# Mixer weights in sections of 512 columns through all ring tiles, parameters earlier on SyncE's queue, narrow products in one run

## The chip, the cores and the metric

The kernel runs on one core of a Trainium2 chip. The metric is device time in microseconds. The runs of the kernel before took 1303.86, 1306.07 and 1306.61 us; the median is 1306.07.

## The reference, cut to what matters

One sequence of 256 tokens, width 1024, with 16 meta tokens in front, goes through a first block (a mixer and a mixture of experts) and then a second block of two layers. The change touches the first block's mixer alone:

```python
a = rmsnorm(h, g_mix)
proj = a @ w_in                       # 1024 x 3584: seven sections of 512 columns
sb_q, sb_k, sb_v, hg_q, hg_f, hg_i, hg_g = split(proj)
o_sb = merge_heads_norm(stick_breaking_attention(sb_q, sb_k, sb_v), sb_gain)
log_f = log(lb + (1 - lb) * sigmoid(hg_f)); k_in = (1 - lb) * sigmoid(-hg_f)
o_hg = merge_heads_norm(hgrn2(silu(hg_q), k_in, hg_i, log_f), hg_gain) * silu(hg_g)
h = h + concat(o_sb, o_hg) @ w_out    # 1024 x 1024
m = rmsnorm(h, g_ffn)
h = h + moe(m)                        # 32 experts: gate, up 1024 x 512; down 512 x 1024
```

Everything is float32. The weights of the 32 experts are 201 MB and all are read.

## The kernel before, in words

**Engines and order.** The program is written in Python on a layer that puts in the semaphores and orders the instructions of each engine by priority and readiness; `tc.issue_after(i)` adds an order behind an instruction. A DMA waits on the queue of the engine that issues it (SyncE, `nc.sync`, for nearly all) until the place of its destination is free, and what is behind it on that queue waits too.

**Places for weights.** `K.ring` is a pool of four tiles of 128 x 4096 floats (2 MB); `wtile()` (L53) takes the next. Five further "boost" tiles (`boost`, L249) are opened one after the other as the mixer's memory comes free: the first at once, the second when `p3` closes (`hg_done`, L570), the third when `p4` closes (L593), two more when `p2` has closed and the `w_out` loop is at n = 3.

**Expert stream.** `expert_stream` (L663) lists all expert loads of 2 MB in the order of use; `fetch(n)` (L685) issues those up to number n, `take()` issues one more and hands out the next. Loads 3 to 7 go to boost tiles, load 9 (RING + BOOST) to a spare tile, load 13 (`mem`) to a pool of its own, all others to the ring.

**Mixer weights.** One ring tile, `qtile`, holds four quarters of 512 KB. A quarter is 128 columns of a `w_in` section (rows of 512 bytes), for sections 2 and 5 two blocks of 128 rows with 512 columns (2 KB), for `w_out` one block of 128 rows (4 KB). `refill` (L125) issues the next quarter. `weights()` (L158) splits quarter after quarter into a high part (a ScalarE cast, L74) and the rest (VectorE or, for `POOLED`, GpSimd, L75), then refills; at the quarters of `AHEAD` it also fetches expert loads 1 to 4. `parts()` hands out one split and has the next one made. Sections come in the order 4, 3, 6, 0, 1, 2, 5.

**Products.** `proj_T` (L281) handles five sections: per 128 columns 24 products of the split weights with the split activations `ah`, `al`. `proj_N` (L296) handles sections 2 and 5: in each of four turns and for each of two blocks kk, 12 wide products (512 columns) and then four narrow ones of the meta tokens (`am`, 32 columns of weights, each with two records in the trace) with the unsplit weights `wt`, added over eight blocks into four regions of the bank `pm`. After each piece `fill()` runs the next bit of `work`: the bias table (`biases`, L1216, which ends in a store of 2.3 MB, `skew`, on ScalarE's queue), the levels of hgrn2 (`lev_prep`, `lev_mm`) and the stick-breaking attention (`sb_z`, `sb_corr`, `sb_exp`, `sb_pv`).

**Small parameters.** `prm` (four small vectors), `rb` and `oh` are loaded on SyncE's queue into tiles of pool `a2`, which opens after the norm (L238 to 246); `parameters()` (L262) transposes `prm` on TensorE after the first piece's products. `cmk` (the level masks) is also loaded on SyncE's queue (L349).

## Time and profile before

| | |
|---|---|
| median of 3 runs | 1306.07 us |
| profiled execution | 1305.46 us |
| its span, first to last instruction | 1303.8 us |
| TensorE (matmul) busy | 1097.9 us, 84% |
| VectorE / ScalarE / GpSimd busy | 641.0 / 454.1 / 65.2 us |
| moved by DMA | 336.54 MB, mean 258 GB/s |
| mean granted TensorE clock | 0.941 |

The profile of one execution has a page of totals, views that group instructions or waits, and timelines. In a timeline a row is one instruction or several alike in a row: start in us from the span's start, length, engine (PE is TensorE, PEld its weight loads, DVE VectorE, ACT ScalarE, POOL GpSimd, SP SyncE; a q behind it means its queue, where DMAs are issued), line, operation, out<-in tiles, shape, count, and in brackets the idle time before it and what ended that. In the view of stretches each engine's busy time stands with the number of its instructions, then the granted clock as a share of full speed, the mean busy share of 16 DMA engines, and GB/s.

### The profile page before, as it was taken

The numbers are of one execution on the slowest core, as the hardware profiler recorded it, in microseconds if no ns is written. First come the engines' busy times: TensorE is split into PE (matmuls) and PEld (weight loads), VectorE is DVE, ScalarE is ACT, GpSimd is POOL, SyncE is SP. The second block draws the span as 40 slices with busy tenths as digits, with TensorE's granted clock in tenths as the row PEclk, the third lists the DMA queues.
The fourth block names the chain that finished last, engine by engine and source line by source line (L and its number), as shares of the span: only waits on it lengthen the run. The fifth ranks groups of instructions, "written<-read, shape, count | busy, mean of one in ns | idle before, by whom it ended". The sixth has DMA issues, their size and how long they took to land. (4 is left out here: it accounts for less than half of the span.)

```text
span 1303.8 us, 18742 instructions
## 1 busy us (share of the span) xinstructions
PE 1097.9 (84%) x7773; PEld 798.5 (61%) x7773; DVE 641.0 (49%) x1225; ACT 454.1 (35%) x808; POOL 65.2 (5%) x109
## 2 busy tenths in 40 slices
PE   8859998767565756646589899999999999999997
PEld 7856674314121412101058668999998887999996
DVE  6646355311021101101037876877677766886676
ACT  5526542101001000000035564444453654544442
POOL 7201000000000000000000001000001000000001
PEclk9979999988888888888799999999998999999999
DMA  8676677999999999999999105555446334365430
GB/s 219 148 173 234 226 292 288 403 406 408 409 409 405 409 409 409 409 409 409 409 370 351 66 4 191 201 219 195 162 151 210 121 133 175 124 243 192 184 118 33
DMA packets 132593, 336.54 MB, mean 258 GB/s; under 512 B 4837, under 2 KB 41294, under 8 KB 132504
## 3 DMA queue, kind: packets, MB, share of 16 engines
q1 hardware_dynamic: 128796, 327.32, 66.4%
q10 hardware_dynamic: 1724, 2.95, 1.8%
q0 software_dynamic: 1984, 5.04, 1.3%
q8 instruction: 62, 1.02, 0.3%
q14 instruction: 27, 0.22, 0.0%
HBM read 331.88 MB, written 3.41 MB: 257 GB/s over the span
## 5 line engine op out<-in xcount | busy, mean ns | idle before, releaser
L75 DVE TENSOR_TENSOR wl<-wt,wh 128x1024 fp32r<-128x1024 f32 x212 | 258.0, 1219 | 111.1 <-ACT wh L74 106.1
L74 ACT CAST wh<-wt 128x1024 fp32r<-128x1024 f32 x216 | 223.9, 1042 | 179.4 <-PE ps L48 134.4
L48 PE MATMUL ps<-xl,wh 128*128 128x256 f32 (+1 forms) x912 | 255.7, 280 | 2.2 <-DVE xl L1434 1.8
L48 PE MATMUL ps<-xh,wh 128*128 128x256 f32 (+1 forms) x912 | 257.0, 282 | 0.4 <-ACT xh L1097 0.3
L48 PE MATMUL ps<-xh,wl 128*128 128x256 f32 (+1 forms) x912 | 255.3, 280 | 0.0
L48 PE MATMUL ps<-wt,xe 128*32 128x512 f32 x944 | 138.9, 720 | 94.9 <-DMA wt<-in_w_expert_up_dram 57.4
L48 PEld LDWEIGHTS ps<-xl,wh 128*128 128x128 f32 (+1 forms) x912 | 171.2, 188 | 4.4 <-POOL xl L1434 2.2
L48 PEld LDWEIGHTS ps<-xh,wh 128*128 128x128 f32 (+1 forms) x912 | 171.2, 188 | 3.4 <-issue 0.8
L48 PEld LDWEIGHTS ps<-xh,wl 128*128 128x128 f32 (+1 forms) x912 | 171.0, 188 | 0.1
L48 PEld LDWEIGHTS ps<-wt,xe 128*32 128x32 f32 x944 | 28.3, 122 | 194.7 <-DMA wt<-in_w_expert_up_dram 73.8
L48 PE MATMUL ps<-wt,hT 128*32 128x512 f32 x496 | 78.6, 766 | 54.0 <-DMA wt<-in_w_expert_down_dram 48.4
L1006 DVE TENSOR_TENSOR hs<-hs,ps 128x512 f32<-128x512 f32 x8 | 5.5, 688 | 224.4 <-PE ps L48 216.0
L1028 DVE TENSOR_TENSOR h<-h,ps 128x512 f32<-128x512 f32 x32 | 22.0, 687 | 145.2 <-PE ps L48 145.2
L48 PEld LDWEIGHTS ps<-wt,hT 128*32 128x32 f32 x496 | 15.6, 129 | 106.5 <-DMA wt<-in_w_expert_down_dram 68.1
L1005 ACT ACTIVATE hs<-ps 128x512 f32<-128x512 f32 x8 | 4.8, 597 | 184.4 <-PE ps L48 184.4
L48 PE MATMUL ps<-wh,gh 128*128 128x512 f32 x176 | 68.6, 390 | 0.0
L48 PE MATMUL ps<-wh,gl 128*128 128x512 f32 x176 | 68.5, 389 | 0.0
L48 PE MATMUL ps<-wl,gh 128*128 128x512 f32 x176 | 68.4, 389 | 0.0
L1040 ACT COPY ye<-ps 128x512 f32<-128x512 f32 x14 | 8.2, 586 | 161.9 <-PE ps L48 161.9
L48 PE MATMUL ps<-ah,wh 128*128 128x256 f32 (+1 forms) x160 | 43.2, 302 | 14.4 <-ACT wh L74 13.9
L2006 ACT CAST gh<-cv 128x256 fp32r<-128x256 f32 x44 | 17.9, 407 | 74.7 <-DVE cv L2003 74.7
L48 PE MATMUL ps<-al,wh 128*128 128x256 f32 (+1 forms) x160 | 42.6, 298 | 0.0
(478 smaller groups left out, 1688.1 us busy)
## 6 DMA issues: line engine op xcount, KB each, us to landing
wt<-in_w_expert_gate_dram SPq DMA_DIRECT2D x30, 2048.0 KB, 17.4
wt<-in_w_expert_down_dram SPq DMA_DIRECT2D x30, 2048.0 KB, 17.9
wt<-in_w_expert_up_dram SPq DMA_DIRECT2D x29, 2048.0 KB, 17.0
wt<-in_ffn_w_in_dram SPq DMA_DIRECT2D x20, 2048.0 KB, 7.8
wt<-in_ffn_w_out_dram SPq DMA_DIRECT2D x10, 2048.0 KB, 10.3
wt<-in_w_in_dram SPq DMA_DIRECT2D x28, 512.0 KB, 3.8
bt<-in_w_expert_up_dram SPq DMA_DIRECT2D x3, 2048.0 KB
wt<-in_shared_w_kv_dram SPq DMA_DIRECT2D x3, 2048.0 KB, 13.5
```

Source lines behind the costliest of these rows:

```text
L48: return nc.tensor.matmul(o, a, b, start=start, stop=stop, skip_group_check=True)
L74: nc.scalar.copy(wh, src)
L75: on.tensor_tensor(out=wl, in0=src, in1=wh.bitcast(F32), op=ALU.subtract)
L1005: nc.scalar.activation(hs, pgu[0], AF.Silu)
L1006: V.tensor_tensor(out=hs, in0=hs, in1=pgu[1], op=ALU.mult)
L1028: V.tensor_tensor(out=hs_, in0=hs_, in1=py, op=ALU.add)
L1040: nc.scalar.copy(ye[:, hf], pd[hf])
L2006: nc.scalar.copy(gh, c)
```

## The change

The mixer's weights come in whole sections of 512 columns (one ring tile each, 2 MB; the first in two halves, `w_out` in two tiles of two loads each) and pass through all four ring tiles; `section()` issues one, four at the start and one more whenever the four pieces of a section have been split. A helper `chain` issues these, `gm`, the small parameters and the first ten expert loads on SyncE's queue in the order written. The small parameters are asked for behind the first half section, into a tile that shares the place of `qT`. Expert load 0 goes to the first boost tile behind the fourth section; 2, 4, 5, 6 go to the other boost tiles (`BOOSTED`) and 1, 3, 7, 8 to the ring. `cmk` is loaded from ScalarE's queue. In `proj_N` the narrow products of all eight blocks stand in one run behind all wide ones; in `sb_corr` and `sb_pv` the narrow products of both halves likewise.

```diff
--- before.py
+++ after.py
@@ -17,7 +17,6 @@
 DRAM = bass.MemoryType.DRAM
 D = 1024
-AHEAD = (18, 21, 23, 25)
 POOLED = (0, 12, 14, 16)
 EPS = 1e-6
 LEVELS = (64, 32, 16, 8, 4, 2, 1)
@@ -81,6 +80,16 @@
         for _ in range(n):
             mm(ps[:, 384:512], K.ident, K.ident, True, True)
+    loads = []
+
+    def chain(dst, src):
+
+        with ExitStack() as es:
+            if loads:
+                es.enter_context(tc.issue_after(loads[-1]))
+            loads.append(nc.sync.dma_start(dst, src).ins)
+
+    K.chain = chain
     K.nbehind = 0
     K.pulse = pulse
     K.mm, K.bank, K.wtile, K.rpow, K.split = mm, bank, wtile, rpow, split
@@ -108,7 +117,7 @@
     nc.scalar.preload_act_table_set("sigmoid_and_others")
     expert_stream(K)
     gm = e1.tile([8, 128], F32, name="gm")
-    nc.sync.dma_start(gm, I["g_mix"].rearrange("o (c p) -> (o c) p", p=128))
+    K.chain(gm, I["g_mix"].rearrange("o (c p) -> (o c) p", p=128))
     rb = a1.tile([33, NH], F32, name="rb")
     V.memset(rb, 1e30)
@@ -116,22 +125,39 @@
     w_out = I["w_out"][0].rearrange("(k p) f -> p k f", p=128)
-    quarters = [w_in[:, :, 512 * s + 128 * c:512 * s + 128 * c + 128] if s not in (2, 5) else
-                w_in[:, 2 * c:2 * c + 2, 512 * s:512 * s + 512] for s in (4, 3, 6, 0, 1, 2, 5) for c in range(4)]
-    quarters += [w_out[:, k:k + 1] for k in W_OUT]
-    qtile = K.wtile()
-    views, loads = [], []
-
-    def refill():
-        n = len(views)
-        if n < len(quarters):
-            q = quarters[n]
-            v = qtile[:, 1024 * (n % 4):1024 * (n % 4) + 1024].rearrange("p (a b) -> p a b", a=q.shape[1])
-            loads.append(nc.sync.dma_start(v, q))
-            views.append(v)
-
-    for _ in range(4):
-        refill()
+
+    views = []
+    chain = K.chain
+    small = a1.tile([128, 4, 256], F32, name="small", tag="qT").rearrange("p a b -> p (a b)")
+    prm, oh = small[0:24, 0:128], small[0:33, 256:640]
+
+    def parameters_in():
+        for o, n, src in ((0, 8, "lb_logits"), (8, 4, "sb_gain"), (12, 4, "hg_gain"), (16, 8, "g_ffn")):
+            chain(prm[o:o + n], I[src].rearrange("o (c p) -> (o c) p", p=128))
+        chain(rb[0:32], I["rel_bias_2"])
+        chain(oh, I["c_rel"])
+
+    def section():
+        n = len(views) // 4
+        t = K.wtile()
+        if n < 7:
+            s = (4, 3, 6, 0, 1, 2, 5)[n]
+            v = t.rearrange("p (k f) -> p k f", k=8)
+            src = w_in[:, :, 512 * s:512 * s + 512]
+            for cs in ((slice(0, 256), slice(256, 512)) if n == 0 else (slice(0, 512),)):
+                chain(v[:, :, cs], src[:, :, cs])
+                if cs.start == n == 0:
+                    parameters_in()
+            views.extend(v[:, 2 * c:2 * c + 2] if s in (2, 5) else v[:, :, 128 * c:128 * c + 128] for c in range(4))
+        else:
+            v = t.rearrange("p (k f) -> p k f", k=4)
+            for j in range(2):
+                k = W_OUT[4 * (n - 7) + 2 * j]
+                chain(v[:, 2 * j:2 * j + 2], w_out[:, k:k + 2])
+            views.extend(v[:, k] for k in range(4))
+
+    for _ in range(2):
+        section()
     negtri = a1.tile([128, 128], F32, name="negtri")
@@ -159,11 +185,11 @@
         for n in range(28):
             v = views[n]
             yield split(v, v.shape[1:], on=nc.gpsimd if n in POOLED else V), v
-            if n < 20:
-                refill()
-            if n in AHEAD:
-                with tc.issue_after(loads[-1].ins):
-                    K.fetch(AHEAD.index(n) + 1)
+            if n % 4 == 3:
+                if n < 23:
+                    section()
+                else:
+                    K.fetch(2 if n == 23 else 4)
         yield None
     stream = weights()
@@ -236,20 +262,17 @@
     mixh, mixl = ah[:, :, 16:272], al[:, :, 16:272]
     a2 = p2.enter_context(tc.tile_pool(name="a2", bufs=2))
-    prm = a2.tile([24, 128], F32, name="prm", tag="wA")
-    oh = a2.tile([33, 384], F32, name="oh", tag="wB")
     ohr = a2.tile([33, 384], F32R, name="ohr", tag="wA")
     tb = a2.tile([NH, 384], F32, name="tb", tag="wB")
-    for o, n, src in ((0, 8, "lb_logits"), (8, 4, "sb_gain"), (12, 4, "hg_gain"), (16, 8, "g_ffn")):
-        nc.sync.dma_start(prm[o:o + n], I[src].rearrange("o (c p) -> (o c) p", p=128))
-    nc.sync.dma_start(rb[0:32], I["rel_bias_2"])
-    nc.sync.dma_start(oh, I["c_rel"])
+    for _ in range(2):
+        section()
     K.boost, K.boostp = ExitStack(), []
     def boost(n):
         K.boostp += n * [K.boost.enter_context(tc.tile_pool(name=f"boost{len(K.boostp)}", bufs=n, side="right"))]
     boost(1)
+    K.fetch(1)
     p3, p4 = ExitStack(), ExitStack()
     a3 = p3.enter_context(tc.tile_pool(name="a3", bufs=1, side="right"))
@@ -298,8 +321,10 @@
         V.memset(dstm, 0.0)
         po = [bank() for _ in range(2)]
         pm = bank()
+        wts = []
         for kp in range(4):
             (wh, wl), wt = parts()
+            wts.append(wt)
             for kk in range(2):
                 k = 2 * kp + kk
                 for t in range(2):
@@ -307,13 +332,13 @@
                     mm(po[t], ah[:, k, ts], wh[:, kk], k == 0, False)
                     mm(po[t], al[:, k, ts], wh[:, kk], False, False)
                     mm(po[t], ah[:, k, ts], wl[:, kk], False, k == 7)
-                for j in range(4):
-                    mm(pm[32 * j:32 * j + 32, 0:128], am[:, k], wt[:, kk, 128 * j:128 * j + 128], k == 0, k == 7)
-            refill()
             if kp < 3:
                 fill()
         for t in range(2):
             nc.scalar.copy(dst[:, t], po[t])
+        for k in range(8):
+            for j in range(4):
+                mm(pm[32 * j:32 * j + 32, 0:128], am[:, k], wts[k // 2][:, k % 2, 128 * j:128 * j + 128], k == 0, k == 7)
         for j in range(4):
             V.tensor_copy(dstm[32 * j:32 * j + 32, j], pm[32 * j:32 * j + 32, 0:128])
         fill()
@@ -346,7 +371,7 @@
     proj_T(16, evac_silu(hq))
     proj_T(16, evac_silu(sg))
     cmk = a3.tile([128, 7, 64], F32, name="cmk")
-    nc.sync.dma_start(cmk, I["c_lev"].rearrange("p (l j) -> p l j", l=7))
+    nc.scalar.dma_start(cmk, I["c_lev"].rearrange("p (l j) -> p l j", l=7))
     with tc.issue_after(getattr(last[-1], "ins", last[-1])):
         tab = nc.scalar.preload_act_table_set("natural_log_exp_and_others")
@@ -523,6 +548,7 @@
                 mm(zA[u].rearrange("p (i t) -> p i t", i=2)[:, :, 128:256], negone,
                    spB[u][:, 0:256].rearrange("p (i t) -> p i t", i=2), False, True)
                 mm(zB[u][:, 0:256], negtri, spB[u][:, 0:256], False, True)
+            for u in range(2):
                 for i in range(2):
                     cs = slice(32 * (2 * qd + i), 32 * (2 * qd + i) + 32)
                     mm(zB[u][cs, ci], negone[:, 0:32], spA[u][:, 256 * i:256 * i + 256], False, False)
@@ -561,8 +587,10 @@
                 for u in range(2):
                     hd = 2 * c + u
                     mm(o_[u][:, 128:256], sv[:, 1, 64 * hd:64 * hd + 64], wB[u][:, 128 * i:128 * i + 128], False, False)
+            for i in range(2):
                 for u in range(2):
-                    mm(o_[u], svm[qs, c, 64 * u:64 * u + 64], wB[u][qs, ci], False, True)
+                    mm(ob[64 * u:64 * u + 64, 256 * i:256 * i + 256], svm[qs, 2 * qd + i, 64 * u:64 * u + 64],
+                       wB[u][qs, ci], False, True)
             return norm_mix(nc, bank, mm, a2, ob, bd64, epsr, [sbg[:, 2 * qd + i:2 * qd + i + 1] for i in range(2)],
                             None, mixh, mixl, 2 * qd)
         return f
@@ -570,7 +598,7 @@
     def hg_done():
         p3.close()
         boost(1)
-        K.fetch(5)
+        K.fetch(3)
     work += [[hg_scan], [hg_inter], [hg_inter_mm, lev_prep(0)], [lev_mm(0)],
              [lev_prep(1)], [lev_mm(1), lev_prep(2)], [lev_mm(2)], [lev_prep(3)],
@@ -592,7 +620,7 @@
     rest.pop(0)()
     p4.close()
     boost(1)
-    K.fetch(6)
+    K.fetch(5)
     rest.pop(0)()
     behind.close()
@@ -604,8 +632,7 @@
     parts = {}
     for n, k in enumerate(W_OUT):
         dst = [K.mpre.tile([128, 1024], F32R, name=f"wo{x}", tag=f"wo{x}") for x in "hl"] if n == 7 else None
-        parts[k] = split(views[28 + n].rearrange("p a (b c) -> p (a b) c", b=2), (2, 512), dst)
-        refill()
+        parts[k] = split(views[28 + n].rearrange("p (b c) -> p b c", b=2), (2, 512), dst)
         if n == 3:
             boost(BOOST - 3)
             K.fetch(3 + BOOST)
@@ -658,6 +685,7 @@
 BOOST = 5
+BOOSTED = (0, 2, 4, 5, 6)
 def expert_stream(K):
@@ -686,8 +714,8 @@
         while len(tiles) < min(n, len(seq)):
             i = len(tiles)
             s = seq[i]
-            if 3 <= i < 3 + BOOST:
-                t = K.boostp[i - 3].tile([128, 4096], F32, name="bt", tag="bt")
+            if i in BOOSTED:
+                t = K.boostp[BOOSTED.index(i)].tile([128, 4096], F32, name="bt", tag="bt")
             elif i == K.RING + BOOST + 4:
                 t = K.m2b.tile([128, 4096], F32, name="st", tag="st")
             elif i == K.RING + BOOST:
@@ -695,7 +723,9 @@
             else:
                 t = K.wtile()
             v = t[:, 0:s.shape[1] * s.shape[2]].rearrange("p (a b) -> p a b", a=s.shape[1])
-            if i < len(seq) - 1:
+            if i <= K.RING + BOOST:
+                K.chain(v, s)
+            elif i < len(seq) - 1:
                 nc.sync.dma_start(v, s)
             else:
                 for hs in (slice(0, 512), slice(512, 1024)):
```

## Rows read from the trace of the kernel before

**Rows 1.** Stretches: length, busy (and count) by engine, granted clock, DMA share, GB/s.

```profile
73.15:86.50 13.35, 0.00 (x1) 0.00 (x1) 0.02 (x1) 1.10 (x2) 0.00 (x0) 0.65 0.82 138
86.50:91.60 5.10, 5.10 (x24) 4.98 (x24) 5.10 (x8) 4.20 (x8) 0.00 (x0) 0.58 0.73 241
91.60:95.90 4.30, 4.30 (x57) 4.08 (x56) 4.30 (x7) 1.44 (x2) 0.00 (x0) 1.00 0.75 250
100.00:150.00 50.00, 50.00 (x491) 31.76 (x490) 25.97 (x35) 31.54 (x52) 5.96 (x14) 1.00 0.61 218
200.90:209.00 8.10, 7.57 (x63) 5.79 (x63) 6.66 (x26) 2.71 (x4) 0.00 (x0) 1.00 0.03 11
228.00:655.00 427.00, 272.75 (x1740) 92.95 (x1732) 53.36 (x84) 30.74 (x51) 0.00 (x0) 0.86 1.02 408
```

**Rows 2.** Waits of TensorE, 228 to 640: us in total, times, longest.

```profile
PE ps L48 <- DMA wt<-in_w_expert_up_dram: 54.2, 22, 4.3
```

**Rows 3.** Timeline, TensorE, items 17 and 18: start, length, line, tiles, shape, idle before.

```profile
86.50 0.59 PE L48 MATMUL ps<-ah,wh 128*128 128x272 f32 x1 [13.35 <-ACT wh L74]
...
91.63 1.15 PE L48 MATMUL ps<-kq 128*64 128x64 f32 x32
...
92.71 0.39 PE L48 MATMUL ps<-ah,wh 128*128 128x272 f32 x1
...
95.92 1.15 PE L48 MATMUL ps<-kq 128*64 128x64 f32 x32
```

**Rows 4.** Timeline, ScalarE: the issue of the store and the late cast.

```profile
50.23 1.39 ACTq L1229 DMA_DIRECT2D skew<-tb  x1
...
85.40 1.04 ACT L74 CAST wh<-wt 128x1024 fp32r<-128x1024 f32 x1 [19.58 <-DMA wt<-in_w_in_dram]
```

**Rows 5.** DMA queues, 60 to 80: packets, MB, share of 16 engines.

```profile
q10 hardware_dynamic: 939, 1.44, 69.2%
q1 hardware_dynamic: 775, 0.39, 6.9%
```

**Rows 6.** Timeline, SyncE's queue: the run of `w_in` quarters.

```profile
15.86 76.13 SPq L130 DMA_DIRECT2D wt<-in_w_in_dram  x18
```

**Rows 7.** Timeline, TensorE: the transpose of `prm`.

```profile
17.04 0.21 PE L264 MATMUL ps<-ident,prm 24*128 24x24 f32 x1 [1.23 <-DMA prm<-in_g_ffn_dram]
```

**Rows 8.** Timeline, TensorE: wide products around a narrow group.

```profile
101.30 0.40 PE L48 MATMUL ps<-wl,ah 128*128 128x512 f32 x1
101.62 0.43 PE L48 MATMUL ps<-wt,am 128*32 128x128 f32 x8
101.98 0.50 PE L48 MATMUL ps<-wh,ah 128*128 128x512 f32 x1
102.31 0.39 PE L48 MATMUL ps<-wh,al 128*128 128x512 f32 x1
102.55 0.39 PE L48 MATMUL ps<-wl,ah 128*128 128x512 f32 x1
```

**Rows 9.** Timeline, TensorE: an unbroken run of narrow products.

```profile
62.69 0.45 PE L48 MATMUL ps<-qi,kmA 128*32 128x128 f32 x8 [2.33 <-DVE qi L386]
62.94 0.42 PE L48 MATMUL ps<-qi,kmB 128*32 128x128 f32 x8
```

**Rows 10.** Timeline, TensorE: a run with full weights and 128 columns.

```profile
157.97 0.38 PE L48 MATMUL ps<-S,hv 128*128 128x128 f32 x2
...
158.41 0.39 PE L48 MATMUL ps<-S,hv 128*128 128x128 f32 x2
```

**Rows 11.** Timeline, SyncE's queue: asks for tile 10 (with 11) and tile 14.

```profile
208.13 4.43 SPq L699 DMA_DIRECT2D wt<-in_w_expert_down_dram  x2
...
227.29 0.37 SPq L699 DMA_DIRECT2D wt<-in_w_expert_up_dram  x1
```

**Rows 12.** Timeline, TensorE: the five boost tiles (3 to 7).

```profile
213.66 8.77 PE L48 MATMUL ps<-bt,xe 128*32 128x512 f32 x80
```

**Rows 13.** Instructions on `am`: length ns least/median/most, first and last start.

```profile
L48 PE MATMUL ps<-wt,am x128: 272/285/297, 101.6 to 156.8; 128*32 128x128 f32 x128
```

## Prediction

> **What bounds the kernel now.** Three views, in this order. First the table of stretches: it cuts the span where the work changes character. From 228 to 655 us (the experts) TensorE is busy 272.75 of 427 us while the DMA share is 1.02 at 408 GB/s [rows 1]; the list of waits has TensorE waiting there for expert tiles, one group of three standing for all: 54.2 us in 22 waits [rows 2]. So that stage ends when its bytes have come, and a gain before it counts only if the unbroken stream of loads begins earlier. Ahead of it, in the mixer, the picture is the other way round: from 100 to 150 us TensorE is busy 50.00 of 50 us at a DMA share of 0.61 [rows 1]. There its own pace sets the time, so an idle stretch of TensorE in the mixer is real loss.
>
> Second, the timeline of the mixer shows one such stretch: TensorE stands still for 13.35 us before the product at 86.50, which waits for a ScalarE cast; the cast (85.40) had itself waited 19.58 us for a load of `w_in` [rows 3, 4]. Third, the DMA view says why that load is late. `biases` sends the `skew` store at 50.23 [rows 4]; from 60 to 80 us that queue (q10) holds 69.2% of the engines' time while the weights' queue (q1) moves 0.39 MB in 775 packets, about one packet for each of the store's 939 [rows 5]. SyncE's row for 15.86 to 92 has eighteen quarters of `w_in` asked for one by one [rows 6], since the ring tile holds four quarters and each must be split before its place is filled again. The loads have at most four pieces of lead, and the store takes longer than that.
>
> I count the 28 pieces of `w_in` as items 0 to 27 and the expert loads in order of use as tiles 0 to 13 (tile 13 is `mem`, 1 MB). The product at 86.50 is item 17.
>
> **The change part by part.**
>
> *Sections through all four ring tiles.* Items 0 to 15 are asked for at the start, with tile 0 behind them: some 10.5 MB, 26 us at the 408 GB/s of [rows 1] (the first loads of 1 and 2 KB rows may be slower). Item 16 to 19's section needs only the splits of items 0 to 3, so it follows directly and is there before 45 us even at three quarters of that rate, ahead of the store at 50.23. The section of items 24 to 27 and `w_out` run beside the store, but are wanted only behind items 17 to 23. The 13.35 us go [rows 3]. What is late next? The cast before the stalled one ended some 20 us earlier, so casts and VectorE halves of item 17 come while TensorE still has item 16; they hide. [...] **Together 15.3 us**; at least 13.35 if the lower clock only moves elsewhere.
>
> *Small parameters first.* TensorE waits 1.23 us for `prm` at 17.04 [rows 7]; the six small loads now come right behind the first half section, so this goes. Against it the first piece to land is 1 MB, not 0.5 MB: at most 1.3 us at 408 GB/s, at least nothing, because the first split is only needed after the transposes and activations of the norm. I take 0.3. **Net 0.9 us**, between -0.1 and 1.2. `cmk`'s load moves to ScalarE's queue: one issue, bounded by the 1.39 us of the `skew` issue [rows 4] and by nothing; ScalarE has long idle stretches, so I take nothing. SyncE itself loses 24 of 36 issues for `w_in` and `w_out`; its new waits are for ring tiles. Behind the wait of tile 1 (for `sv`'s narrow products) stand only further expert tiles, wanted when the experts begin.
>
> *Narrow products behind the wide ones.* In `proj_N` each `kk` ends with eight records of 128x32 weights. Wide products start 0.24 us apart (102.31 to 102.55); from 101.30 to 102.31, two wide steps and one narrow group, it is 1.01, so a group costs 1.01 - 0.48 = 0.53 us [rows 8]. Eight records of exactly this shape in an unbroken run take 0.25 us (`kmA` at 62.69 to `kmB` at 62.94) [rows 9]; the other 0.28 is the way in and out. Eight groups now cost 4.2 us; in one run 8 x 0.25 + 0.28 = 2.3. That saves 1.96 in each of two `proj_N`, **3.9 us**, on a stretch where TensorE is never idle [rows 1]. Bounds: a run could be slower because no wide product stands in front of its weight loads. The nearest row of a run with full 128x128 weights and the same 128 columns has 0.11 us a record (four from 157.97 to 158.41) [rows 10]: 64 x 0.11 + 0.28 = 7.3, a loss of 3.1 in each, 6.2 in all. I take the 3.9, from the row of the same shape. `sb_corr` and `sb_pv`, twice each, lose one way in and out: 0 to 0.28 each, I take **0.4 us** for the four.
>
> [...]
>
> *Expert tiles in other places.* Before, tiles 0, 1, 2 lie in the ring and tiles 3 to 7 in the boost buffers; after, tiles 1, 3, 7 lie in the ring and 0, 2, 4, 5, 6 in boost. Tiles 10, 11, 12 take over the ring places of the three, so they can be asked for only when tiles 1, 3, 7 are used. Before, tile 10 is asked for at 208.13 and the ask for tile 14, when tile 8 is used up, comes at 227.29 [rows 11], when the 7.3 MB of tiles 10 to 13, 18 us, have just gone through. Tile 7 is used up with the five boost tiles at 213.66 + 8.77 = 222.43 [rows 12]. Asking for tile 12 only then leaves 3 MB (tiles 12, 13), 7.7 us, ahead of tile 14: it starts at 222.43 + 7.7 = 230.1 where it started at 227.3. **2.8 us lost**, between nothing and the 5.1 us of one tile. The loads ahead of the experts still fit: from the close of `p4` on they are six tiles instead of five and the last 1 MB of `w_out`, 1 MB or 2.6 us more, and the queue is idle (share 0.03) from 200.90 to 209 [rows 1].
>
> **Sum.** 15.3 + 0.9 + 3.9 + 0.4 - 2.8 = 17.7 us. The profiled execution took 1305.46 us (span 1303.8), 0.6 below the median of 1306.07 shown: 1287.8 on its own scale, **1288.4** on the median's. Nothing behind the experts depends on absolute time, so the shift stays.
>
> **The rivals.** (1) *A narrow run does not hide its weight loads:* 0.11 us a record, 6.2 lost instead of 3.9 won: 1298.5. [...] Against: [rows 9]. (2) *VectorE takes the place of the load.* From 91.6 to 95.9 it is busy 4.30 of 4.30 us beside a TensorE also at 4.30 [rows 1]: no reserve. If items 17 to 20 each waited a quarter of that, 4.3 us: 1292.7. Against: without the stall VectorE starts these items several us ahead of TensorE. (3) *The change doesn't do what it says:* the section of item 17 slips behind the `skew` store. [...] Against: it is there before 45. (4) *No change:* the expert stream cannot start earlier because the tiles ahead of it were themselves at the limit of the queue; the mixer's gain turns into a wait: about 1306. Against: share 0.61 and 0.03 in [rows 1]. (5) *Slower:* in a run each narrow product waits for the one before it, as all add to the same four regions of one bank: 0.285 us, the full length of one record [rows 13], 64 x 0.285 + 0.28 = 18.5 instead of 4.2, 28.6 lost in all in place of 3.9 won: 1320.9. It decides from 0.17 us a record, where the 13.8 us of the other terms are used up (64 x 0.17 + 0.28 = 4.2 + 6.9). Against: wide products add to one bank too, 0.24 apart at 0.39 long [rows 8].
>
> **How the numbers follow.** Forecast 0.68; (1) 0.11; (2) 0.09; (3) 0.04; (4) 0.04; (5) 0.04. The forecast's own bounds: best 15.3 + 1.2 + 3.9 + 1.1 - 0 = 21.5 (1284.6). Downward the unknown costs of the narrow run [rows 9, 10] and the ring order reach to rivals (1) to (3). The range from 1283 to 1298 leaves out half of (1), and (4) and (5). A difference of 0.2% (2.6 us) is about what a measurement of this kernel can tell from none. Faster: the first four cases, 0.92; within 0.2%: 0.04; slower: 0.04.
>
> **What would show it.** In the profile after: no wait of a mixer cast for `w_in` near 85; full granted clock at the items behind it; no wait for `prm`; 64 narrow records in a row in about 2 us; the first expert product some 20 us earlier; tile 12 asked for only when the boost tiles are used up, and the unbroken stream some 17 us earlier than before. The forecast is wrong if a narrow run takes over 5 us, if TensorE shows new waits for VectorE between 60 and 100, or if the stream's start moves by less than the mixer's end minus three us.

## The result and the profile after

| | before | after |
|---|---|---|
| median of the runs, us | 1305.41 (1303.86 to 1306.61, 4 runs) | 1289.36 (1289.07 to 1289.44, 4 runs) |
| ratio | | 0.9873, 95% interval 0.9861 to 0.9886 |
| profiled execution: time, span, us | 1305.46, 1303.8 | 1289.3, 1287.6 |

The change makes the kernel 16.1 us faster. (The median before was 1306.07 with the three runs that the prediction starts from; a fourth, 1304.76, makes it 1305.41.) A second set of runs of the changed kernel (`e5_after_again`, below) gave 1287.5, so single medians carry 1 to 2 us of scatter; where the parts are told apart below, the timelines do it, not the medians. The profiled span is 16.2 us shorter. To see where that comes from, the span is cut at instructions that both kernels have. The first fence is TensorE's timeline of the kernel after, the second that of the kernel before at the places not yet shown (the others are in [rows 3, 9 and 11]); columns as in [rows 3].

```profile
47.87 0.34 PE L47 MATMUL ps<-ohr,rh 33*12 33x384 f32 x1
...
61.09 0.68 PE L47 MATMUL ps<-qi,kmA 128*32 128x128 f32 x8 [2.34 <-DVE qi L411]
...
68.14 1.15 PE L47 MATMUL ps<-kq 128*64 128x64 f32 x16
...
72.33 0.29 PE L47 MATMUL ps<-ah,wh 128*128 128x272 f32 x1
...
75.43 1.15 PE L47 MATMUL ps<-kq 128*64 128x64 f32 x32
...
147.19 0.24 PE L1270 MATMUL ps<-ident,pe 32*128 32x32 f32 x1
...
184.85 1.92 PE L47 MATMUL ps<-bt,xe 128*32 128x512 f32 x16
...
190.12 1.92 PE L47 MATMUL ps<-wt,xe 128*32 128x512 f32 x16
```

```profile
49.10 0.34 PE L48 MATMUL ps<-ohr,rh 33*12 33x384 f32 x1
...
68.79 1.15 PE L48 MATMUL ps<-kq 128*64 128x64 f32 x16
...
167.57 0.24 PE L1240 MATMUL ps<-ident,pe 32*128 32x32 f32 x1
...
205.19 1.92 PE L48 MATMUL ps<-wt,xe 128*32 128x512 f32 x16
```

| point in the program | before | after | gained so far | gained since the last point |
|---|---|---|---|---|
| `ohr` (behind item 11) | 49.10 | 47.87 | 1.23 | 1.23 |
| `kmA` | 62.69 | 61.09 | 1.60 | 0.37 |
| first `kq` (behind item 15) | 68.79 | 68.14 | 0.65 | -0.95 |
| `kq` behind item 17 | 91.63 | 75.43 | 16.20 | 15.55 |
| `pe` (mixer's projections done) | 167.57 | 147.19 | 20.38 | 4.18 |
| first expert product | 205.19 | 184.85 | 20.34 | -0.04 |
| ask for tile 10 | 208.13 | 192.10 | 16.03 | -4.31 |
| end of the span | 1303.8 | 1287.6 | 16.2 | 0.2 |

The row at 72.33, item 17's first product, has no bracket behind it: the 13.35 us of [rows 3] are gone, and item 17 takes 75.43 - 72.33 = 3.10 us at a granted clock of 1.00, where it took 5.13. Two entries are clearly negative. The first, -0.95, goes with the granted clock, in the table of stretches (columns as in [rows 1]), the kernel after first and then the kernel before:

```profile
61.10:63.00 1.90, 1.90 (x20) 1.52 (x21) 1.90 (x3) 1.90 (x4) 0.09 (x1) 0.50 0.71 74
63.00:66.00 3.00, 3.00 (x16) 3.00 (x16) 2.81 (x4) 0.97 (x3) 3.00 (x1) 0.50 0.85 113
66.00:68.00 2.00, 2.00 (x16) 2.00 (x15) 1.30 (x1) 0.68 (x1) 0.21 (x1) 0.82 0.87 142
```

```profile
62.69:65.00 2.31, 2.31 (x25) 2.11 (x26) 2.31 (x4) 2.30 (x5) 0.48 (x1) 0.68 0.71 74
65.00:68.00 3.00, 3.00 (x20) 3.00 (x20) 2.81 (x3) 0.59 (x1) 2.82 (x1) 0.68 0.68 74
```

TensorE stands still for 2.34 us while VectorE makes `qi`; behind that the granted clock is 0.50 up to 66 and 0.82 from 66 to 68. Before, behind a wait of 2.33 us [rows 9], it was 0.68 on the mean from 62.69 to 68. The second, -4.31, is the ask for tile 10, in SyncE's timeline:

```profile
192.10 3.80 SPq L729 DMA_DIRECT2D wt<-in_w_expert_down_dram  x2
202.41 0.37 SPq L729 DMA_DIRECT2D wt<-in_w_expert_gate_dram  x1
...
206.64 0.37 SPq L729 DMA_DIRECT2D wt<-in_w_expert_up_dram  x1
```

Before, it came 208.13 - 205.19 = 2.94 us behind the first expert product; after, 192.10 - 184.85 = 7.25. The place that tile 10 takes is that of tile 1, and tile 1's products are those at 190.12, which end at 192.04.

The mixer's end moved by 20.34 us where the terms ahead of the experts made 20.5, and the stream by 16.03 where some 17 were forecast. From 212 us on the experts are as they were, bound by their bytes: the stretch and the longest group of waits that answer [rows 1] and [rows 2] are, for the kernel after,

```profile
212.00:640.00 428.00, 277.46 (x1696) 92.61 (x1694) 53.49 (x84) 29.92 (x50) 0.00 (x0) 0.82 1.03 408
```

```profile
PE ps L47 <- DMA wt<-in_w_expert_up_dram: 53.3, 23, 3.2
```

with the share at 1.03 and 408 GB/s, so what reaches the end is what moves the stream of loads.

### The profile page after: what moved, and what is told of

It is laid out like the page before. It is cut to its first block, busy times and chain, and to the rows that moved or that the text cites. A ratio compares the mean times of both kernels' runs of the same rounds, so it can differ in the third digit from the quotient of the medians.

```text
span 1287.6 us, 18701 instructions
## 1 busy us (share of the span) xinstructions
PE 1099.2 (85%) x7773; PEld 799.2 (62%) x7773; DVE 642.1 (50%) x1225; ACT 453.3 (35%) x808; POOL 66.0 (5%) x109
## 5 line engine op out<-in xcount | busy, mean ns | idle before, releaser
L47 PE MATMUL ps<-wt,xe 128*32 128x512 f32 x944 | 143.5, 740 | 92.0 <-DMA wt<-in_w_expert_up_dram 53.3
## 6 DMA issues: line engine op xcount, KB each, us to landing
wt<-in_w_expert_up_dram SPq DMA_DIRECT2D x31, 2048.0 KB, 15.3
```

What stands on the lines that cost most here:

```text
L47: return nc.tensor.matmul(o, a, b, start=start, stop=stop, skip_group_check=True)
```

## The experiments

Four theories were to be told apart. For the stall: the store holds up the loads, or four quarters are too little lead in any case. For the narrow run: it saves, or it doesn't hide its weight loads. For the expert tiles: the places cost something, and by which tile. For the small parameters: order, or size of the first load. The table puts all runs side by side (the ratio is to the kernel before on the same chip; "experts" is the span less the start of the first expert product).

| run | median us | ratio, 95% interval | span | first expert product | experts | ask for tile 10 |
|---|---|---|---|---|---|---|
| before | 1305.4 | | 1303.8 | 205.19 | 1098.6 | 208.13 |
| after | 1289.4 | 0.9873 (0.9861 to 0.9886) | 1287.6 | 184.85 | 1102.8 | 192.10 |
| `e1_ring_first` | 1286.2 | 0.9850 (0.9832 to 0.9868) | 1284.3 | 184.84 | 1099.5 | 188.04 |
| `e2_store_late` | 1287.6 | 0.9863 (0.9846 to 0.9879) | 1286.0 | 187.10 | 1098.9 | 190.03 |
| `e3_narrow_back` | 1290.6 | 0.9880 (0.9863 to 0.9898) | 1289.5 | 187.91 | 1101.6 | 195.18 |
| `e4_s4_behind_store` | 1288.9 | 0.9879 (0.9859 to 0.9898) | 1283.9 | 183.82 | 1100.1 | 191.08 |
| `e5_after_again` | 1287.5 | 0.9864 (0.9848 to 0.9880) | 1285.3 | 183.76 | 1101.5 | 191.01 |
| `e6_small_late` | 1289.9 | 0.9876 (0.9860 to 0.9892) | 1283.9 | 184.24 | 1099.7 | 191.50 |
| `e7_s4_waits` | 1305.3 | 0.9999 (0.9989 to 1.0008) | 1303.4 | 202.00 | 1101.4 | 209.27 |
| `e8_best` | 1288.0 | 0.9858 (0.9842 to 0.9874) | 1287.6 | 187.82 | 1099.8 | 191.02 |
| `e9_after_late` | 1285.9 | 0.9849 (0.9835 to 0.9864) | 1287.3 | 184.00 | 1103.3 | 191.27 |
| `e10_best_late` | 1283.8 | 0.9838 (0.9824 to 0.9852) | 1281.6 | 182.41 | 1099.2 | 185.61 |
| `e11_best_late_pulse` | 1283.1 | 0.9831 (0.9817 to 0.9845) | 1284.0 | 183.59 | 1100.4 | 186.80 |
| `e12_sb_back` | 1288.3 | 0.9863 (0.9842 to 0.9885) | 1288.4 | 185.81 | 1102.6 | 193.07 |

### The store, taken out of the way in the kernel before

```diff
-    nc.scalar.dma_start(K.scratch, tb.unsqueeze(1).to_broadcast([NH, 128, 384]))
+    K.tbd = K.dram.tile([NH, 384], F32, name="tbd")
+    nc.scalar.dma_start(K.tbd, tb)
...
+    work[12].append(lambda: nc.scalar.dma_start(K.scratch, K.tbd.unsqueeze(1).to_broadcast([NH, 128, 384])))
```

> The kernel before, with one edit: the 2.4 MB skew store is sent after item 24 of the mixer's weights (all of w_in asked for by then), from a small copy of tb in DRAM; quarters, ring and order of the loads stay. Theory (the store takes the DMA engines from the loads of w_in): the stall of 13.35 us at item 17 and the low clock behind it go, 1305.4 - 15.3 = 1290.1, up to 1293 if the store now delays w_out or an expert tile. Rival (a ring of four quarters has too little lead with or without the store): the stall stays, 1305 (1303 to 1306).

Measured: 1287.6, 18 us less than before and 2.5 less than the theory gave. TensorE's and ScalarE's timelines, and the DMA queues from 64 to 75 us (columns as in [rows 5]):

```profile
61.72 0.45 PE L48 MATMUL ps<-qi,kmA 128*32 128x128 f32 x8 [2.33 <-DVE qi L386]
...
66.25 1.14 PE L48 MATMUL ps<-kq 128*64 128x64 f32 x16
...
73.56 1.15 PE L48 MATMUL ps<-kq 128*64 128x64 f32 x32
```

```profile
63.52 0.86 ACTq L580 DMA_DIRECT2D skew<-tbd  x1
```

```profile
q10 hardware_dynamic: 1377, 2.12, 51.1%
q1 hardware_dynamic: 1316, 1.06, 33.3%
```

From the first `kq` to the one behind item 17 it is 7.31 us, where it was 22.84: no stall, with the same ring of four quarters and the same order of loads. The rival of too little lead is out. Two things differ from what was expected. The store was sent at 63.52, not behind item 24: ScalarE's queue did not keep to the place in the program text here, and the last quarter of `w_in` was asked for only at 108.18. And read from DRAM it moves 1377 of its 1536 packets (2304 KB in rows of 1.5 KB) in 11 us, 65 ns each (51.1% of 16 engines for 11 us, by 1377). From `tb` it is 381 packets in 8 us at 237 ns each (the last fence of this document), so some 32 us in all. So this run does not separate "later" from "shorter"; it shows that the store as it was caused the stall. The gain beyond 15.3 lies ahead of it: `kmA` comes 0.97 us earlier (61.72 instead of 62.69), and from there to the first `kq` it is 4.53 us instead of 6.10.

That kernel holds none of the change's edits and is as fast as the changed one.

### The sections, put behind the store

The first attempt only moved the calls in the program:

```diff
-            if n % 4 == 3:
-                if n < 23:
-                    section()
-                else:
-                    K.fetch(2 if n == 23 else 4)
+            if n in (12, 13, 14, 15, 19):
+                section()
+            if n in (23, 27):
+                K.fetch(2 if n == 23 else 4)
```

> The changed kernel with the fifth to seventh section of w_in asked for at items 12, 13 and 15 instead of 3, 7 and 11: that is behind the skew store, with the ring places long free. Theory (each packet of the loads waits for one of the store): item 16's section is 1024 packets, at 775 packets in 20 us 26 us, from 51 to 77; TensorE wants item 16 at 69.2 and gets it near 78.5: 9.3 us of stall and some 2 us of low clock, 1300.6 (1297 to 1303). Rival (the store is no hindrance to a load of 2 MB): it lands in 5 to 6 us, near 57, no stall, 1289.4.

Measured: 1288.9, with no stall, but the run says nothing on either theory: in SyncE's timeline the three sections are asked for when their ring places come free, from 23.5 us on, as in the kernel after (23.46, 20.61, x3).

```profile
23.53 20.50 SPq L90 DMA_DIRECT2D wt<-in_w_in_dram  x3
```

SyncE's queue ran ahead of the place in the program text: all three were asked for by 44.03, before ScalarE sent the store (48.97). The second attempt gave it a wait: a copy of one element into the section's tile, which ScalarE does behind the issue of the store.

```diff
+            if n == 4:
+                with tc.issue_after(K.stored):
+                    nc.scalar.copy(t[0:1, 0:1], tb[0:1, 0:1])
```

> The changed kernel, with the load of the fifth section (items 16 to 19) made to wait for a one-element copy that ScalarE does behind the issue of the skew store, near 51, and the later sections behind it: now the load really goes behind the store, which the earlier attempt (items 12, 13 and 15 in program order alone) did not do. Theory (one packet of the load for one of the store): 1024 packets at about 190 in 4 us, 22 us, or 26 us by 775 in 20 us; it lands between 73 and 77, item 16 is wanted at 69.2 and starts between 74.5 and 78.5, with some 2 us of low clock behind it: 7 to 11 us more, 1298 (1295 to 1301). Rival (a load of 2 MB is not held up): 1289.4.

Measured: 1305.3, above the 1295 to 1301 of the theory: the time of the kernel before, 17.8 us more than the changed kernel in the same set. Timelines of SyncE, ScalarE and TensorE, and the DMA queues from 51 to 83 us:

```profile
50.65 30.06 SPq L90 DMA_DIRECT2D wt<-in_w_in_dram  x3
```

```profile
83.84 1.04 ACT L73 CAST wh<-wt 128x1024 fp32r<-128x1024 f32 x1 [21.89 <-DMA wt<-in_w_in_dram]
```

```profile
84.93 0.60 PE L47 MATMUL ps<-ah,wh 128*128 128x272 f32 x1 [16.72 <-ACT wh L73]
```

```profile
q10 hardware_dynamic: 1463, 2.25, 60.6%
q1 hardware_dynamic: 1351, 2.73, 23.4%
```

The store does hold up a load of 2 MB, and harder than expected: the section is asked for at 50.65 and used at 83.84, 33 us and not 22 to 26. The counts tell that "one packet for one" was too kind. The two queues moved nearly as many packets (1351 and 1463), but the section has only 1024 of the 1351: at least 327 belong to loads asked for behind it, and they moved while the section was still wanted. Why they went ahead is not shown: the view doesn't part the packets by engine, and a count by queue doesn't tell when the last packet of one load came.

So big sections and a ring of four tiles are worth nothing by themselves here. What they buy is that items 16 to 27 are asked for before the store is.

### The narrow products, back in their groups

```diff
+                for j in range(4):
+                    mm(pm[32 * j:32 * j + 32, 0:128], am[:, k], wt[:, kk, 128 * j:128 * j + 128], k == 0, k == 7)
...
-        for k in range(8):
-            for j in range(4):
-                mm(pm[32 * j:32 * j + 32, 0:128], am[:, k], wts[k // 2][:, k % 2, 128 * j:128 * j + 128], k == 0, k == 7)
```

> The changed kernel with the narrow products of proj_N back behind each kk's wide ones. Theory (a run saves the way in and out of each group): from the two traces, summed over both proj_N, wide and narrow products together take 34.6 us before and 31.2 after without a wait of 0.53, so 3.4 us slower: 1292.8 (1292 to 1293.5; the prediction's own figure of 3.9 gives 1293.3). First rival of the prediction (a run doesn't hide its weight loads and costs 6.2): faster, 1283.2. Rival (the mixer's gain is swallowed by the wait for expert tiles): 1289.4.

Measured: 1290.6, below the 1292 to 1293.5 of the theory and 1 to 3 us more than the changed kernel, too close for the medians. TensorE's timeline is sharper:

```profile
68.06 1.15 PE L47 MATMUL ps<-kq 128*64 128x64 f32 x16
...
150.28 0.24 PE L1269 MATMUL ps<-ident,pe 32*128 32x32 f32 x1
```

From the first `kq` to `pe` it is 82.22 us; in the changed kernel 79.05 (147.19 - 68.14), and 79.08 in `e5_after_again`. The run is worth **3.2 us**. It would be 3.7, but with the run TensorE waits 0.53 us for ScalarE's `sq` further on, a wait that is not in this kernel. The theory had left that wait out. The first rival (dearer, 1283.2) is out, and the gain is passed on: first expert product 3.1 us later, ask for tile 10 3.1 us later.

### sb_corr and sb_pv in their old order

```diff
-            for u in range(2):
                 for i in range(2):
                     cs = slice(32 * (2 * qd + i), 32 * (2 * qd + i) + 32)
...
+                for u in range(2):
+                    mm(o_[u], svm[qs, c, 64 * u:64 * u + 64], wB[u][qs, ci], False, True)
```

> The changed kernel with the products of sb_corr and sb_pv back in the order of the kernel before. Theory from the two traces: sb_corr's products take 12.6 us there and 12.2 here (both calls), sb_pv 2.76 and 2.46 a call, so the regrouping gives 1.0 us; from the first product on kq to the transposes of pe 80.1 us instead of 79.05 to 79.1, and the time 1 us more (within what the times can tell): 1289.5 (1287 to 1291.5). Prediction's own figure: 0.4 us, 79.5. Rival (the order doesn't matter): 79.1.

Measured: 1288.3, no difference that the medians show. From the first `kq` (68.49) to `pe` (148.19) it is 79.70 us: 0.65 more than the changed kernel, between the 79.5 of the prediction and the 80.1 of the theory. The wait for `sq` shrinks at the same time from 0.53 to about 0.2, so the products themselves lose some 1.0 us and the wait takes 0.3 of it back.

### The small parameters behind the whole first section

```diff
-                if cs.start == n == 0:
-                    parameters_in()
+            if n == 0:
+                parameters_in()
```

> The changed kernel with the six small parameters asked for behind both halves of the first section instead of behind the first half. Theory (their place in the queue gave the 1.2 us that TensorE no longer waits for prm): 1.2 us more at the first products, which the mixer passes on: 1290.6. Rival (prm lands in time either way, and the gain came from the larger first loads): the transposes of the parameters don't wait, 1289.4. Whether TensorE waits for small (prm) is read from the trace, as 1 us is near what the times can tell.

Measured: 1289.9, not to be told from the changed kernel. TensorE's timeline, and then SyncE's of this kernel and of the kernel before:

```profile
13.74 0.23 PE L287 MATMUL ps<-ident,small 24*128 24x24 f32 x1 [0.59 <-DMA small<-in_g_ffn_dram]
```

```profile
7.26 0.29 SPq L90 DMA_DIRECT2D small<-in_g_ffn_dram  x1
```

```profile
12.33 0.37 SPq L130 DMA_DIRECT2D wt<-in_w_in_dram  x1
12.82 0.41 SPq L244 DMA_DIRECT2D prm<-in_lb_logits_dram  x1
```

TensorE waits 0.59 us, and `ohr` comes at 48.20 instead of 47.87: the order is worth 0.33 us, not the 1.2 of the theory; and TensorE does wait, against the rival. The other 0.9 of the change's 1.23 us at `ohr` don't come from the order. The timelines point to another wait that is gone: before, the loads stood in SyncE's queue behind the fifth quarter (12.33), which had waited 1.8 us for the first quarter's split; here they are asked for by 7.26 even behind the whole section. No run parts that wait from the larger first loads.

### The expert tiles that are used first, in the ring

```diff
-BOOSTED = (0, 2, 4, 5, 6)
+BOOSTED = (3, 4, 5, 6, 7)
+ORDER = (3, 0, 4, 1, 5, 6, 7, 2)
...
+            i = ORDER[i] if i < len(ORDER) else i
```

> The changed kernel with the expert tiles in other places: tiles 0, 1, 2 (used first) in the ring, 3 to 7 in the boost buffers, each place filled at the same moment as in the changed kernel. Theory from the trace of after: tile 10 is asked for at 192.10, when tile 1 is used up (its products end at 192.04), 7.25 us after the first expert product (184.85); in the kernel before it was 2.94 us after it (208.13 against 205.19). With tile 0 in the ring the ask comes 4.3 us earlier, near 187.8, and the whole stream with it: 1289.4 - 4.3 = 1285.1 (1284.4 to 1286.0). The prediction's own mechanism (tile 12 waits for tile 7, 2.8 us): 1286.6, with the ask for tile 10 where it is. Rival (the stream is bound by its bytes further back, places don't matter): 1289.4.

Measured: 1286.2. TensorE's and SyncE's timelines:

```profile
184.84 1.92 PE L47 MATMUL ps<-wt,xe 128*32 128x512 f32 x16
```

```profile
188.04 4.43 SPq L731 DMA_DIRECT2D wt<-in_w_expert_down_dram  x2
...
208.04 0.37 SPq L731 DMA_DIRECT2D wt<-in_w_expert_up_dram  x1
```

The first expert product stands where it stood (184.84), and the ask for tile 10 comes 4.06 us earlier (188.04 against 192.10), as the theory from the trace said: it was tile 1's place, not tile 7's. The time alone would not show it: it lies just outside the 1284.4 to 1286.0 of the theory, and the 1286.6 of the prediction's own mechanism is as near.

Not all of the 4.06 us arrives. Tile 14 is asked for at 208.04, later than in the changed kernel (206.64), though the stream began sooner; by then the loads asked for are through, and the stream has a hole. Stretches of `e1_ring_first` and then of the changed kernel (columns as in [rows 1]):

```profile
208.00:210.00 2.00, 2.00 (x17) 0.45 (x12) 0.00 (x0) 0.00 (x0) 0.00 (x0) 0.61 0.64 203
```

```profile
208.00:210.00 2.00, 2.00 (x24) 0.65 (x20) 0.00 (x0) 0.00 (x0) 0.00 (x0) 1.00 1.03 412
```

All six executions with tiles 0 to 2 in the ring have such a hole some 20 us behind the ask for tile 10, and a smaller one 7 us behind it. Counted in stretches of 1 us against 408 GB/s, the stream lacks 1.4 to 3.0 us of bytes in the 36 us from 2 us behind that ask on, 2.6 on the mean. In the eight executions with the changed kernel's places it lacks 0.1 to 0.7, 0.3 on the mean. So the changed places ask 4.1 us later, but leave 2.3 us fewer holes.

The column "experts" has six executions with tiles 0 to 2 in the ring (before, `e1`, `e2`, `e8`, `e10`, `e11`: 1098.6 to 1100.4, mean 1099.4) and eight with the changed kernel's places (1099.7 to 1103.3, mean 1101.6). The places cost **2.2 us** on the mean, near the 1.8 that this leaves, with a scatter in the single execution that is nearly as large.

### The changed kernel once more, and with the store read from DRAM

> The changed kernel once more, unchanged, beside the others of this set, so that differences of 1 to 3 us can be read against runs on the same chip: 1289.4, within 2 us.

Measured: 1287.5, inside what was expected. In the first version of the store from DRAM it follows its copy at once, and tiles 0 to 2 are in the ring:

```diff
-    nc.scalar.dma_start(K.scratch, tb.unsqueeze(1).to_broadcast([NH, 128, 384]))
+    K.tbd = K.dram.tile([NH, 384], F32, name="tbd")
+    nc.scalar.dma_start(K.tbd, tb)
+    nc.scalar.dma_start(K.scratch, K.tbd.unsqueeze(1).to_broadcast([NH, 128, 384]))
```

> The changed kernel with expert tiles 0, 1, 2 in the ring (as in the run with other places) and the skew store read from a small copy of tb in DRAM, at its old place in the program. Theory: the places give 3 us (3.3 in the spans of that run), and the store from DRAM, 65 ns a packet where it took 235, ends within some 10 us, so that items 12 to 17 run as in the run with the late store, 1 to 2.7 us faster (the first expert product then near 182.5 instead of 184.85): 1289.4 - 3 - 2 = 1284.4 (1282.5 to 1286.5). Rival (the mixer of the changed kernel doesn't feel the store any more): 1286.4.

Measured: 1288.0, 3.6 more than the theory gave and not better than the changed kernel. ScalarE's timeline:

```profile
50.61 0.56 ACTq L1262 DMA_DIRECT2D tbd<-tb  x1
...
54.98 0.86 ACTq L1263 DMA_DIRECT2D skew<-tbd  x1
55.89 1.62 ACT L393 ACTIVATE lf<-lf,lb,omlb 128x272 f32<-128x272 f32 x3 [2.45 <-DMA tbd<-tb]
```

ScalarE waits 2.45 us for its own copy to land before it can send the store, and the activations behind it are on the path: `kmA` comes at 65.01 instead of 61.09. The second version sends the store later, with the edit of `e2_store_late`; the third puts the early tiles in the ring as well; the fourth fills TensorE's wait ahead of `kmA`:

```diff
+        K.pulse(20, pm)
```

> The changed kernel with the skew store read from a small copy of tb in DRAM and sent where the run with the late store sent it (near 63, once the copy has long landed, so that ScalarE doesn't wait for it). Theory: items 12 to 17 gain what they gained there (qi to kq 4.5 us instead of 5.9 to 7.1 in the changed kernel, and ScalarE's wait goes), 1 to 2 us; first expert product near 182.3 (183.8 and 184.85 in the two looks at the changed kernel), 1288.5 - 1.5 = 1287 (1285 to 1288.5). Rival (with the sections ahead of the store the store costs nothing): 1288.5, first expert product 183.8 to 184.9.

> The same, and expert tiles 0, 1, 2 in the ring. Theory: tile 10 is asked for 2.9 to 3.2 us after the first expert product (near 185.3, where the changed kernel does it at 191.0 to 192.1), of which some 2 us are lost again in the stream, whose 8 groups took 444.4 us from that ask on with tiles 0 to 2 in the ring and 442.1 with the changed kernel's places: 2 us less than the run before this, 1285 (1283 to 1286.5). Rival (the places give nothing in the end): as the run before this.

> The same, and 20 products on the identity (no use is made of them) ahead of the products on kmA, to fill the 2.33 us in which TensorE waits for qi. Theory (the low granted clock behind that wait, 0.50 from 61.09 to 66.00 in the changed kernel, comes from the idle stretch): the clock stays at 1.00 and the stretch from qi to kq falls to 4.5 us; where the run before this one already shows 4.5 there, nothing is gained: 1283.5 to 1285. Rival (the clock falls at this place whatever TensorE does in the 2.33 us): no difference, 1285.

Measured: 1285.9, 1283.8 and 1283.1. `e10_best_late` and `e11_best_late_pulse` are faster than both kernels: their intervals lie below that of the changed kernel in the result, and that of the second also below the one of `e5_after_again`, which the first still touches. `e9_after_late` can't be told from the changed kernel by its time. The tiles in the ring give 2.1 us between the medians here (1285.9 to 1283.8), with intervals that overlap. What the shorter store gives hangs on the clock, one stretch of which is shown for `e5_after_again`, `e9_after_late`, `e10_best_late` and `e11_best_late_pulse`, in this order:

```profile
63.00:66.00 3.00, 3.00 (x23) 3.00 (x23) 2.81 (x4) 0.96 (x3) 3.00 (x1) 0.80 0.86 116
```

```profile
63.00:66.00 3.00, 3.00 (x16) 3.00 (x16) 2.81 (x4) 0.83 (x2) 2.58 (x1) 0.50 0.65 172
```

```profile
63.00:66.00 3.00, 3.00 (x28) 2.87 (x28) 2.81 (x4) 0.99 (x3) 2.58 (x1) 1.00 0.64 158
```

```profile
63.00:66.00 3.00, 3.00 (x29) 3.00 (x27) 2.52 (x3) 0.96 (x2) 2.45 (x1) 1.00 0.87 276
```

`e9` and `e10` have the same program up to here and the same idle stretch of 2.3 us; one has 0.50 from 63 to 66, the other 1.00, and from `kmA` to the first `kq` that is 6.05 against 4.51 us. With the idle stretch filled it is 4.50 at a clock of 1.00; but the 20 products take longer than the wait they fill, `kmA` comes at 62.38 instead of 61.23, and no gain is left that the times show. The rival that the clock falls there whatever TensorE does has nothing for it, but one execution of each doesn't exclude chance.

## Why the prediction was right

The forecast was 1288.4 and the measurement 1289.36. All five terms of the sum came out within 0.7 us of their size, the last one on the mean over many executions; one of them had the wrong mechanism, and one a reason that was only half right. Of the 1.6 us that the gain is short of the forecast's 17.7, the clock behind `qi` has 0.95; and in this pair of executions the experts take 4.2 us longer (1098.6 and 1102.8), not 2.2.

One of the prediction's own signs of being wrong came: the start of the stream moved by 16.03 us, less than the mixer's end (20.34) minus three. It points at the term of the expert tiles, below; the other two signs didn't come.

*Sections, 15.3.* Measured 15.55 between the two `kq`. Cause, place and clock were right: no cast waits for `w_in`, and the 1.95 by which 15.3 exceeds 13.35 is what the low clock had cost: before, item 17 took 5.13 us at 0.58 on the mean and item 18, the same 24 products, 3.21 at 1.00 [rows 1, 3]; after, item 17 takes 3.10 at 1.00. What is late next was not asked widely enough: the idle stretch at `qi` ahead of it, 2.33 us before [rows 9] and 2.34 after, has the low clock behind it for longer in this execution (0.50 up to 66), and 0.95 is lost there. "At least 13.35 if the lower clock only moves elsewhere" had allowed for that.

*Small parameters, 0.9.* Measured 1.23 at `ohr`. The term was right as a wait that goes; its reason was half right (0.33 order, the rest by the timelines the fifth quarter's wait ahead of them).

*Narrow products, 3.9.* Measured 3.2, or 3.7 without the new wait for `sq`. The pace was read from the right row; TensorE after, and then its weight loads on `am`:

```profile
105.44 0.39 PE L47 MATMUL ps<-wl,ah 128*128 128x512 f32 x1
105.76 1.95 PE L47 MATMUL ps<-wt,am 128*32 128x128 f32 x64
107.64 0.50 PE L47 MATMUL ps<-wh,ah 128*128 128x512 f32 x1
107.98 0.40 PE L47 MATMUL ps<-wh,al 128*128 128x512 f32 x1
```

```profile
L47 PEld LDWEIGHTS ps<-wt,am x128: 106/110/110, 105.8 to 136.5; 128*32 128x32 f32 x128
```

64 records start in 1.88 us, 0.029 us each (0.031 by [rows 9]). From 105.44 to 107.98, less two wide steps, the run costs 2.1 us with the way in and out, where 2.3 was predicted. The step that was mis-sized is the claim of a stretch without idle time: shortening TensorE's work by 2 us brought it up against ScalarE's `sq`, 0.53 us. The row of the second fence has the length of a weight load, 106/110/110 ns least, median and most: loads that long in a run at 29 ns a record must overlap; how they do no run here shows. Rivals (1) and (5) fall with the pace of the run.

*sb_corr and sb_pv, 0.4.* Measured 1.0 in the products, 0.65 in the path.

*Expert tiles, -2.8.* Measured -2.2 on the mean, but the step that said why is wrong. It had tile 12 waiting for tile 7. Tile 12 is indeed asked for only at 202.41, when tile 7 is used up, and that costs little: the DMA share stays between 0.94 and 1.04 from 194 to 210 us, first with tiles 10 and 11, and none of the eight executions with these places lacks more than 0.7 us in its stream. What was overlooked is tile 10: its place passed from tile 0, used first, to tile 1, whose products come behind the gather at 190.12. That is 4.31 us at the ask, of which about half comes back in holes that the stream no longer has. That the net of these is near the 2.8 us of a wait that costs little is luck.

*Rivals.* (2) VectorE in the load's place: not seen; the one new wait, 0.53 us, is for ScalarE. (3) The section behind the store: not what the change does, but `e7_s4_waits` built it. It costs 17.8 us, more than the 7 to 11 of that run's theory, whose price came from a count of packets by queue. (4) The stream that can't start earlier: only the 4.31 us.

That the store is what stalls the kernel before was argued from two queues' shares [rows 5]; `e2_store_late` and `e7_s4_waits` show it from both sides. Still open: what makes the smaller hole 7 us behind the ask for tile 10, and what decides whether the clock falls behind the wait for `qi`.

## What to carry to other kernels

When a load is late, look at which other queue holds the DMA engines before you change the loads: moving one store, read from DRAM, gave as much (1287.6 us) as rebuilding the whole weight path (1289.4 and 1287.5). Where buffers are reused in turn, the tiles that are used first belong in the places that are refilled first, and the cost of another order is followed through all refills: here 4.1 us at the first, of which holes in the stream take back 2.3. A gain on a busy engine is worth its length only up to the next engine's work (here 3.7 became 3.2), and a DMA that had to wait for another one held up the engine that issues it (ScalarE, 2.45 us in `e8_best`).

## What was not expected of the hardware

The store from `tb`, alone on the DMA engines, moves 74 GB/s and still keeps 70.7% of their time; from 56 to 64 us in the kernel after:

```profile
q10 hardware_dynamic: 381, 0.59, 70.7%
q1 hardware_dynamic: 1, 0.00, 0.1%
```

The same bytes read from a copy in DRAM (`e2_store_late`) went at 2.12 MB in 11 us beside other loads, 193 GB/s, with 51.1% of the engines' time. The packets have the same size (1.5 KB: 0.59 MB in 381, 2.12 MB in 1377) and the same destination; only the place that they are read from differs. `tb` lies in 12 partitions; no run here put it in others, so why it is read at 74 GB/s is not shown.

Behind one and the same idle stretch of 2.3 us, TensorE's granted clock from 63 to 66 us was 0.50 (after, `e9_after_late`), 0.80 (`e5_after_again`) and 1.00 (`e10_best_late`); between `e9` and `e10` it goes with 1.5 us, 6.05 against 4.51. In a kernel with such a place, 1 us between two executions says little without the clock beside it.
